# A post-norm decoder trunk on one core: the layer norms' statistics kept in PSUM, and the last norm in tile pairs

## The chip, the core and the metric

The kernel runs on one core of a Trainium2 chip. The core has five engines that work side by side: TensorE (PE in the rows; PEld is its weight load), VectorE (DVE), ScalarE (ACT), GpSimd (POOL) and SyncE (SP), which here issues the DMAs. Each engine takes its instructions strictly in the order in which they stand, and engines wait for each other through semaphores. Tiles lie in SBUF or, where TensorE writes its results, in the banks of PSUM. The metric is the device time of one execution in microseconds; lower is better.

## The reference

Two post-norm layers on x (256 tokens by 2048 features, float32): an RWKV-7 time mixing, a gated MLP, a causal differential attention, a gated MLP. Each of these four is followed by a layer norm.

```python
def layer_norm(x, g, b):
    mu = x.mean(-1, keepdims=True)
    var = jnp.square(x - mu).mean(-1, keepdims=True)
    return (x - mu) * lax.rsqrt(var + LN_EPS) * g + b

for i in range(DEPTH):                       # DEPTH = 2
    h = rwkv7_mix(x, ...) if i % 2 == 0 else diff_attn_mix(x, ...)
    x = layer_norm(ALPHA * x + h, ln_g[i, 0], ln_b[i, 0])
    x = layer_norm(ALPHA * x + conv_glu(x, ...), ln_g[i, 1], ln_b[i, 1])
```

## The kernel before

Activations lie transposed: features on the 128 partitions, the 256 tokens along a row. `X` holds the residual as 16 tiles of 128x256 (KT = 16). Every dense product is made in split precision. A weight chunk `raw` (128x512) comes by DMA; ScalarE rounds it to `hi` (L213), VectorE takes the rest `lo = raw - hi` (L216), each over 128x256, that is two k-tiles of 128. The activation is split the same way into `S` (L194 on ScalarE, L195 on VectorE). TensorE multiplies hi by both halves and lo by the high half (L228, L229, or in three narrow pieces). So a `lo` is wanted for every two k-tiles, and TensorE can run ahead of VectorE only as far as finished `lo` tiles reach.

The sums of a norm are made on TensorE by a product with a constant matrix (L348), into the two halves of one PSUM bank `lnst`: the mean in `sx`, the mean square in `sq`. `ln_stats` then lets ScalarE square the mean into `ln_m2` (L422) and copy the mean to SBUF as `ln_dm` (L423), VectorE form the variance `ln_v` (L424), ScalarE take Ln and Exp (L322, L323), and VectorE refine the result in three instructions (L324 to L326, a Newton step) into `ln_rs`, in SBUF.

The first three norms are hidden behind the next dense stage. An `Ahead` object makes the products of that stage's first six weight blocks with the tiles before they are normalized (L899 to L901, 16 k-tiles of six blocks) and mends the result afterwards in `total` with `ln_dm` and `ln_rs` (L307, L309). In between, `ln_apply` normalizes the 16 tiles: GpSimd subtracts the mean from all of them (L438), VectorE multiplies by `ln_rs` (L447, L455 or L460), ScalarE or VectorE applies scale and bias (L448, L456, L461, L462), and the tile is split again (L194, L195). All of this stands on the engines among the L213 and L216 rows of the running products. A scheduler writes the order on each engine out at build time, by its own estimates; nothing is reordered on the chip.

The fourth norm has nothing behind it: `ln_finish` subtracts the mean on VectorE (the tiles in `FIN_V`) and on GpSimd (the others, L475), multiplies by scale and `ln_rs` in one VectorE instruction (L483), adds the bias on ScalarE (L485) and sends two tiles at a time (L487).

Of the kernel before, what the change touches and what calls it, by code (L numbers as in the profile page):

```python
# [8 lines left out]
F32 = mybir.dt.float32  # L9
F32R = mybir.dt.float32r  # L10
AF = mybir.ActivationFunctionType
ALU = mybir.AluOpType
AX = mybir.AxisListType

P = 128
T = 256
D = 2048
KT = D // P
# [20 lines left out]
ORDER = [0, 1, 14, 2, 3, 4, 5, 6, 7, 15, 8, 9, 10, 11, 12, 13]  # L39
DBL = 64 * 16 + 16  # L40
LEAD = dict(q=9, p=(), e=1, a=1, s=4, n=0.301, d=8, h=0.1, r='ACAAAAAAAAAAABBB')
FIN_V = (0, 2, 5, 8, 11, 14)
FIN_S = range(2, KT + 1, 2)


def _param_layout():
# [82 lines left out]
class Trunk:  # L129
# [199 lines left out]
    def ln_begin(self, ahead=None, share=False):  # L329

        if self.ln_st is None:
            mk = lambda name, **k: self.ctx.enter_context(self.tc.tile_pool(name=name, bufs=1, side="right", **k))
            st = mk("lnst", space=bass.MemoryType.PSUM).tile([P, 2 * T], F32, name="lnst")
            self.ln_st = [st[:, :T], st[:, T:]]
            pool = mk("lnp")
            self.ln_dm, self.ln_rs, self.ln_c, self.ln_m2, self.ln_v = (
                pool.tile([P, T], F32, name=f"ln_{n}") for n in ("dm", "rs", "c", "m2", "v"))
            self.ln_sq = pool.tile([P, 4, T], F32, name="ln_sq")
            self.ln_acc = pool.tile([P, 2 * T], F32, name="ln_acc")
        self.ln_n, self.ln_open, self.ln_share, self.ln_first = 0, False, share, []  # L340
        self.ln_ahead, self.ln_last = ahead, []
        if ahead is not None:
            ahead.columns()
# [68 lines left out]
            nc.vector.tensor_tensor(out=x, in0=xa, in1=halves[0], op=ALU.add)  # L412
            self.ln_sums(j, n)

    def ln_stats(self):

        nc = self.nc
        sx, sq = self.ln_st
        self.ln_colsum((self.ln_acc[:, :T], self.ln_acc[:, T:]))
        for n, tiles in enumerate(self.ln_last):  # L420
            self.ln_colsum(tiles, n == len(self.ln_last) - 1)
        nc.scalar.activation(out=self.ln_m2, in_=sx, func=AF.Square)  # L422
        nc.scalar.copy(out=self.ln_dm, in_=sx)  # L423
        nc.vector.scalar_tensor_tensor(out=self.ln_v, in0=sq, scalar=LN_EPS, in1=self.ln_m2, op0=ALU.add,  # L424
                                       op1=ALU.subtract)
        self.rsqrt(self.ln_v, self.ln_rs, T, self.ln_m2)

    def ln_plain(self, i, h):
        self.ln_stats()
# [38 lines left out]

    def ln_finish(self, i, h, out):
        nc = self.nc  # L470
        at = 0

        def center(j):
            eng = nc.vector if j in FIN_V else nc.gpsimd
            eng.tensor_tensor(out=self.X[:, j, :], in0=self.X[:, j, :], in1=self.ln_dm, op=ALU.subtract)  # L475

        for j in range(-2, KT):
            if j < KT - 2:
                center(j + 2)
            if j < 0:  # L480
                continue
            x = self.X[:, j, :]
            nc.vector.scalar_tensor_tensor(out=x, in0=x, scalar=self.p(f"ln_g{i}{h}", j), in1=self.ln_rs, op0=ALU.mult,  # L483
                                           op1=ALU.mult)
            nc.scalar.activation(out=x, in_=x, func=AF.Identity, bias=self.p(f"ln_b{i}{h}", j))  # L485
            if j + 1 in FIN_S:
                nc.sync.dma_start(out=out[:, at:j + 1, :], in_=self.X[:, at:j + 1, :])  # L487
                at = j + 1

    def lead(self, feed, group, *args, ramp=0, ahead=4):  # L490

# [12 lines left out]
    def glu(self, i, lead, ahead=None, out=None):  # L504
        nc, tc = self.nc, self.tc
        with ExitStack() as ctx:
            self.weight_pools(ctx, f"g{i}")
            self.psum_pool(ctx, f"g{i}", 5)
            hp = ctx.enter_context(tc.tile_pool(name=f"glu_h{i}", bufs=1))
            gp_ = ctx.enter_context(tc.tile_pool(name=f"glu_t{i}", bufs=2))  # L510
            hs = hp.tile([P, FT, 2 * T], F32R, name="hs")
            gps = [hp.tile([P, T + 2], F32, name=f"gp{k}") for k in range(2)]
            for g in gps:
                nc.gpsimd.memset(g[:, 0:2], 0.0)
            cpar = hp.tile([P, 4 * FT], F32, name="cpar")
            nc.sync.dma_start(out=cpar, in_=self.a["par"][:, PCOL[f"cw{i}0"]:PCOL[f"cw{i}0"] + 4 * FT])
            cw = lambda k, j: cpar[:, k * FT + j:k * FT + j + 1]
            state = {}

            def evac(idx, ps):  # L520
                j = idx // 2
                if idx % 2 == 0:
                    g = gps[j % 2]
                    self.total(ps, g[:, 2:])
                    gc = gp_.tile([P, T], F32, name="gc")
                    nc.vector.tensor_scalar(out=gc, in0=g[:, 0:T], scalar1=cw(0, j),
                                            scalar2=cw(3, j), op0=ALU.mult, op1=ALU.add)
                    for k in (1, 2):
                        nc.vector.scalar_tensor_tensor(out=gc, in0=g[:, k:k + T], scalar=cw(k, j),
                                                       in1=gc, op0=ALU.mult, op1=ALU.add)  # L530
                    nc.scalar.activation(out=gc, in_=gc, func=AF.Gelu_apprx_tanh)
                    state[j] = gc
                else:
                    u = gp_.tile([P, T], F32, name="u")
                    self.total(ps, u)
                    nc.vector.tensor_tensor(out=u, in0=u, in1=state.pop(j), op=ALU.mult)
                    self.split(u, hs[:, j, :])

            blocks = self.up_blocks(i)
            n = 0  # L540
            if lead:
                n = len(lead.src)
                rest = lead.run(evac, [self.psum() for _ in lead.src])
                next(rest)
                if LEAD["e"] == 0:
                    _all(rest)
            for j, w in enumerate(blocks[n:]):
                def ev(_, ps, j=j):
                    if lead:
                        for _ in range(LEAD["e"]):  # L550
                            next(rest, None)
                    evac(j + n, ps)
                self.dense([w], KT, self.S0, ev)
            todo = self.bias_table() if i == 0 else iter(())
            self.ln_begin(ahead)
            for j in range(KT):
                if j in (1, 3, 5, 7, 9):
                    next(todo, None)
                last = j == KT - 1
                self.dense([self.a["ff_down"][i][j]], FT, hs, lambda _, ps: self.ln_add(j, ps, narrow=last, last=last),  # L560
                           narrow=last)
            if out is not None:
                self.ln_stats()
                self.ln_finish(i, 1, out)
            elif not ahead:
                self.ln_plain(i, 1)
# [366 lines left out]
def _all(steps):  # L933
    for _ in steps:
        pass
# [554 lines left out]
```

## Time and profile before

| | |
|---|---|
| three runs | 2544.0, 2544.87 and 2546.05 us; median 2544.87 |
| profiled execution | 2540.27 us, its span 2537.5 us, granted TensorE clock 0.99 |
| busy, TensorE | 2461.7 us (97%), its weight loads 2170.2 us |
| busy, VectorE / ScalarE / GpSimd | 2030.6 us (80%) / 1648.8 us (65%) / 172.0 us (7%) |
| the norms in the trace (L424 starts) | 662.99, 1394.15, 1793.29 and 2519.05 us |

Matmuls are pipelined, so the busy time of TensorE says little about idle time; the distance between starts does. A row of the timeline has the start, the duration, engine, line, operation, output and inputs, and in brackets how long the engine had been idle and what ended that.

### The profile page before, as it was taken

How to read it: one execution, taken by the hardware profiler on the slowest of the kernel's cores; microseconds unless marked ns; L12 is line 12 of the kernel's file. 1: busy time of each engine (PE TensorE's matmuls, PEld its weight loads, DVE VectorE, ACT ScalarE, POOL GpSimd, SP SyncE). 2: the span in 40 equal slices, each digit the busy share in tenths (PEclk: the TensorE clock that was granted, in tenths of full speed). 3: DMA queues.
4: the chain of work that ended last, by engine and by line, in shares of the span. 5: the costliest groups of instructions: out<-in, count | busy, mean ns of one | idle time of the engine just before them, and what ended most of it. 6: DMA issues, size and time to landing. Idle time of an engine off the chain costs nothing.

```text
span 2537.5 us, 56569 instructions
## 1 busy us (share of the span) xinstructions
PE 2461.7 (97%) x18622; PEld 2170.2 (86%) x18622; DVE 2030.6 (80%) x5192; ACT 1648.8 (65%) x4334; POOL 172.0 (7%) x236
## 2 busy tenths in 40 slices
PE   7999999999899999999999999999999999999996
PEld 6988888777888888888889899988988888888886
DVE  8988888878997777776776977779887777776776
ACT  5766566545676666665666666666766666666664
POOL 1000000000300000000111200003300000000111
PEclk9999999999999999999999999999999999999998
DMA  6644343344465556666766455556465555566664
GB/s 189 187 141 120 110 108 102 106 127 125 133 198 189 190 190 190 190 190 196 215 188 188 149 167 174 171 176 184 147 198 188 188 188 188 188 187 186 188 190 128
DMA packets 276743, 428.70 MB, mean 169 GB/s; under 512 B 60632, under 2 KB 83168, under 8 KB 276448
## 3 DMA queue, kind: packets, MB, share of 16 engines
q1 hardware_dynamic: 276448, 425.10, 55.6%
q8 instruction: 145, 2.38, 0.4%
q14 instruction: 150, 1.23, 0.2%
HBM read 420.25 MB, written 6.31 MB: 168 GB/s over the span
## 4 chain that ended last, share of the span: by engine, by line
PE 81%; DVE 3%; ACT 1%; DMA 1%; issue 1%; SPq 0%; POOL 0%; ACTq 0%; DVEq 0%; POOLq 0%
PE psd L228 43%; PE psd L229 22%; PE psd L224 2%; PE psd L225 2%; PE psd L226 2%; PE psd L296 1%; PE psd L295 1%; PE psd L294 1%; PE psd L900 1%; PE psd L899 1%; PE psd L901 1%; DVE lo L216 1%; DMA raw<-in_rw_o 1%; PE lnst L348 1%; PE pss L1152 0%
## 5 line engine op out<-in xcount | busy, mean ns | idle before, releaser
L213 ACT CAST hi<-raw 128x256 fp32r<-128x256 f32 (+1 forms) x3128 | 1231.4, 404 | 682.1 <-PE psd L228 466.2
L216 DVE TENSOR_TENSOR lo<-raw,hi 128x256 fp32r<-128x256 f32 (+1 forms) x3124 | 1308.3, 430 | 418.9 <-ACT hi L213 375.9
L228 PE MATMUL psd<-S,hi 128*128 128x512 f32 x3004 | 1056.7, 396 | 0.8 <-DVE S L195 0.8
L229 PE MATMUL psd<-S,lo 128*128 128x256 f32 x3004 | 842.1, 280 | 3.9 <-DVE lo L216 3.8
L228 PEld LDWEIGHTS psd<-S,hi 128*128 128x128 f32 x3004 | 566.2, 189 | 132.8 <-ACT hi L213 1.3
L229 PEld LDWEIGHTS psd<-S,lo 128*128 128x128 f32 x3004 | 566.0, 188 | 5.6 <-DVE lo L216 5.3
L228 PE MATMUL psd<-hs,hi 128*128 128x512 f32 x1290 | 451.2, 394 | 0.0
L229 PE MATMUL psd<-hs,lo 128*128 128x256 f32 x1290 | 361.5, 280 | 0.0
L228 PEld LDWEIGHTS psd<-hs,hi 128*128 128x128 f32 x1290 | 241.8, 187 | 56.3 <-ACT hi L213 0.9
L229 PEld LDWEIGHTS psd<-hs,lo 128*128 128x128 f32 x1290 | 243.1, 188 | 0.4 <-DVE lo L216 0.3
L226 PE MATMUL psd<-S,lo 128*128 128x256 f32 x480 | 139.1, 290 | 2.9 <-DVE lo L216 2.8
L224 PE MATMUL psd<-S,hi 128*128 128x256 f32 x480 | 138.5, 289 | 1.6 <-ACT hi L213 1.4
L225 PE MATMUL psd<-S,hi 128*128 128x256 f32 x480 | 137.6, 287 | 0.0
L228 PE MATMUL psd<-S1r,hi 128*128 128x512 f32 x276 | 107.2, 419 | 2.0 <-ACT hi L213 1.0
L226 PEld LDWEIGHTS psd<-S,lo 128*128 128x128 f32 x480 | 90.7, 189 | 8.6 <-DVE lo L216 5.0
L224 PEld LDWEIGHTS psd<-S,hi 128*128 128x128 f32 x480 | 90.7, 189 | 6.4 <-ACT hi L213 2.3
L225 PEld LDWEIGHTS psd<-S,hi 128*128 128x128 f32 x480 | 90.6, 189 | 1.7 <-issue 1.4
L366 POOL COPY ln_acc<-X 128x256 f32<-128x256 f32 x4 | 2.0, 512 | 1239.3 <-DVE X L400 1239.3
L224 PE MATMUL psd<-S1r,hi 128*128 128x256 f32 x284 | 85.6, 301 | 0.0
L900 PE MATMUL psd<-S,lo 128*128 128x258 f32 x256 | 77.7, 303 | 8.1 <-DVE lo L216 8.1
L228 PE MATMUL psd<-S1a,hi 128*128 128x512 f32 x240 | 84.9, 398 | 0.0
L229 PE MATMUL psd<-S1r,lo 128*128 128x256 f32 x276 | 80.8, 293 | 1.5 <-DVE lo L216 1.5
(303 smaller groups left out, 3577.3 us busy)
## 6 DMA issues: line engine op xcount, KB each, us to landing
raw<-in_ff_up SPq DMA_DIRECT2D x676, 256.0 KB, 3.4
raw<-in_ff_down SPq DMA_DIRECT2D x320, 256.0 KB, 3.0
raw<-in_rkv SPq DMA_DIRECT2D x192, 256.0 KB, 3.6
raw<-in_da_qk SPq DMA_DIRECT2D x122, 256.0 KB, 3.4
raw<-in_da_v SPq DMA_DIRECT2D x64, 256.0 KB, 3.0
raw<-in_da_o SPq DMA_DIRECT2D x64, 256.0 KB, 3.7
raw<-in_rw_o SPq DMA_DIRECT2D x50, 256.0 KB, 3.3
raw<-in_ff_down SPq DMA_DIRECT2D x32, 192.0 KB, 2.6
```

Source lines behind the costliest of these rows:

```text
L213: nc.scalar.copy(out=hi[:, :s * P], in_=r)
L216: eng.tensor_tensor(out=lo[:, :s * P], in0=r, in1=hi[:, :s * P].bitcast(F32), op=ALU.subtract)
L224: nc.tensor.matmul(ps[:, :T], lhsT=hi, rhs=xs[:, :T], start=first, stop=False)
L225: nc.tensor.matmul(ps[:, :T], lhsT=hi, rhs=xs[:, T:], start=False, stop=False)
L226: nc.tensor.matmul(ps[:, :T], lhsT=lo, rhs=xs[:, :T], start=False, stop=last)
L228: nc.tensor.matmul(ps, lhsT=hi, rhs=xs, start=first, stop=False)
L229: nc.tensor.matmul(ps[:, T:], lhsT=lo, rhs=xs[:, :T], start=False, stop=last)
L294: nc.tensor.matmul(o, lhsT=xh, rhs=hi, start=k == 0 and b == 0, stop=False)
L295: nc.tensor.matmul(o, lhsT=xh, rhs=lo, start=False, stop=False)
L296: nc.tensor.matmul(o, lhsT=xl, rhs=hi, start=False, stop=k == KT - 1 and b == T // P - 1)
L348: self.nc.tensor.matmul(st, lhsT=self.c("onesd"), rhs=t, start=not self.ln_open and n == 0, stop=stop and n == 1)
L900: nc.tensor.matmul(ps[:, 2:4 + T], lhsT=lo[:, w], rhs=x[:, 2:4 + T], start=False, stop=False)
```

## The change

`ln_begin` gives the names `ln_mean` and `ln_rs` to the two halves of the PSUM bank `lnst`; the SBUF tile for `ln_rs` is gone. `ln_stats` takes an optional function that is called after the variance, and spells out the reciprocal root with the result in that bank: ScalarE's Exp and VectorE's last refining instruction write it there, and the three instructions are written so that each reads the bank as one of its two inputs. Whatever multiplied by `ln_rs` in SBUF (L309, L447, L455, L460) now reads PSUM. GpSimd still subtracts `ln_dm`, the copy in SBUF.

`ln_finish` works on pairs of tiles. First come all subtractions: four pairs on VectorE, 128x512 at a time against `ln_mean` in PSUM, the eight tiles of the pairs in `FIN_P` on GpSimd. They are handed to `ln_stats`, so they stand ahead of Ln and Exp. Then, pair by pair, VectorE multiplies by `ln_rs` (128x512); scale and bias are one instruction per tile, on VectorE for the five tiles in the new `FIN_V` and on ScalarE for eleven. The pairs of `FIN_P` come last. Each pair is sent by itself, eight transfers as before.

```diff
-FIN_V = (0, 2, 5, 8, 11, 14)
-FIN_S = range(2, KT + 1, 2)
+FIN_P = (4, 6, 8, 10)
+FIN_V = (3, 7, 11, 13, 15)
...
-            self.ln_dm, self.ln_rs, self.ln_c, self.ln_m2, self.ln_v = (
-                pool.tile([P, T], F32, name=f"ln_{n}") for n in ("dm", "rs", "c", "m2", "v"))
+            self.ln_dm, self.ln_c, self.ln_m2, self.ln_v = (
+                pool.tile([P, T], F32, name=f"ln_{n}") for n in ("dm", "c", "m2", "v"))
+
+            self.ln_mean, self.ln_rs = self.ln_st
...
-    def ln_stats(self):
+    def ln_stats(self, then=None):
...
-        self.rsqrt(self.ln_v, self.ln_rs, T, self.ln_m2)
+        if then is not None:
+            then()
+        l, rs = self.ln_m2, self.ln_rs
+        nc.scalar.activation(out=l, in_=self.ln_v, func=AF.Ln)
+        nc.scalar.activation(out=rs, in_=l, func=AF.Exp, scale=-0.5)
+        nc.vector.tensor_tensor(out=l, in0=self.ln_v, in1=rs, op=ALU.mult)
+        nc.vector.scalar_tensor_tensor(out=l, in0=l, scalar=-0.5, in1=rs, op0=ALU.mult, op1=ALU.mult)
+        nc.vector.scalar_tensor_tensor(out=rs, in0=l, scalar=1.5, in1=rs, op0=ALU.add, op1=ALU.mult)
...
     def ln_finish(self, i, h, out):
-        for j in range(-2, KT):
-            if j < KT - 2:
-                center(j + 2)
-            ...
-            nc.vector.scalar_tensor_tensor(out=x, in0=x, scalar=self.p(f"ln_g{i}{h}", j), in1=self.ln_rs, op0=ALU.mult,
-                                           op1=ALU.mult)
-            nc.scalar.activation(out=x, in_=x, func=AF.Identity, bias=self.p(f"ln_b{i}{h}", j))
-            if j + 1 in FIN_S:
-                nc.sync.dma_start(out=out[:, at:j + 1, :], in_=self.X[:, at:j + 1, :])
+        wide = lambda t: t.unsqueeze(1).broadcast_to([P, 2, T])
+        g, b = (lambda j: self.p(f"ln_g{i}{h}", j)), (lambda j: self.p(f"ln_b{i}{h}", j))
+
+        def center():
+            for j in range(0, KT, 2):
+                xs = self.X[:, j:j + 2, :]
+                if j in FIN_P:
+                    for k in range(2):
+                        nc.gpsimd.tensor_tensor(out=xs[:, k], in0=xs[:, k], in1=self.ln_dm, op=ALU.subtract)
+                else:
+                    nc.vector.tensor_tensor(out=xs, in0=xs, in1=wide(self.ln_mean), op=ALU.subtract)
+
+        self.ln_stats(center)
+        for j in [j for j in range(0, KT, 2) if j not in FIN_P] + list(FIN_P):
+            xs = self.X[:, j:j + 2, :]
+            nc.vector.tensor_tensor(out=xs, in0=xs, in1=wide(self.ln_rs), op=ALU.mult)
+            for k in (j, j + 1):
+                x = self.X[:, k, :]
+                if k in FIN_V:
+                    nc.vector.tensor_scalar(out=x, in0=x, scalar1=g(k), scalar2=b(k), op0=ALU.mult, op1=ALU.add)
+                else:
+                    nc.scalar.activation(out=x, in_=x, func=AF.Identity, scale=g(k), bias=b(k))
+            nc.sync.dma_start(out=out[:, j:j + 2, :], in_=xs)
```

The new program numbers the lines behind these edits higher by up to 13: L447 of before is L456 after, L455 is L464, L456 is L465. VectorE in the first norm, from the refining instructions on, before (`ln_m` is the tile `ln_m2`):

```order
L324 TENSOR_TENSOR ln_m_9945<-ln_rs 128x256 [waits Activation_49]
L216 TENSOR_TENSOR lo<-raw,hi 128x256 [waits DMAHW0_49,DVE_49,Activation_49]
L325 SCALAR_TENSOR_TENSOR ln_m_9945<-ln_m_9945,ln_v 128x256 [waits DVE_49]
L216 TENSOR_TENSOR lo<-raw,hi 128x256 [waits Activation_49]
L326 SCALAR_TENSOR_TENSOR ln_rs<-ln_m_9945,ln_rs 128x256 [waits DVE_49]
L216 TENSOR_TENSOR lo<-raw,hi 128x256 [waits DMAHW1_49,Activation_49]
L447 TENSOR_TENSOR X<-X,ln_rs 128x256 [waits DVE_49,Pool_49]
L455 TENSOR_TENSOR X<-X,ln_rs 128x256 [waits Pool_49]
L216 TENSOR_TENSOR lo<-raw,hi 128x256 [waits Activation_49]
L456 TENSOR_SCALAR X<-X,par 128x256 [waits DVE_49]
L447 TENSOR_TENSOR X<-X,ln_rs 128x256 [waits Pool_49]
L216 TENSOR_TENSOR lo<-raw,hi 128x256 [waits DMAHW2_49,Activation_49]
```

The same place after, where `lnst` is the PSUM bank:

```order
L433 TENSOR_TENSOR ln_m_9944<-ln_v,lnst 128x256 [waits DVE_49,Activation_49]
L216 TENSOR_TENSOR lo<-raw,hi 128x256 [waits DMAHW0_49,Activation_49]
L434 SCALAR_TENSOR_TENSOR ln_m_9944<-ln_m_9944,lnst 128x256 [waits DVE_49]
L216 TENSOR_TENSOR lo<-raw,hi 128x256 [waits Activation_49]
L435 SCALAR_TENSOR_TENSOR lnst<-ln_m_9944,lnst 128x256 [waits DVE_49]
L216 TENSOR_TENSOR lo<-raw,hi 128x256 [waits DMAHW1_49,Activation_49]
L456 TENSOR_TENSOR X<-X,lnst 128x256 [waits DVE_49,Pool_49]
L464 TENSOR_TENSOR X<-X,lnst 128x256 [waits Pool_49]
L216 TENSOR_TENSOR lo<-raw,hi 128x256 [waits Activation_49]
L465 TENSOR_SCALAR X<-X,par 128x256 [waits DVE_49]
L216 TENSOR_TENSOR lo<-raw,hi 128x256 [waits DMAHW2_49,Activation_49]
L195 TENSOR_TENSOR S_76<-X,S_76 128x256 [waits Activation_49] x2
```

The rows stand almost as before, with other inputs; the second L447 has moved behind the next L216 and two L195 (and a further L216, not shown). In the last norm two more places moved. ScalarE, after, from the copy of the mean on:

```order
L425 COPY ln_dm<-lnst 128x256
L431 ACTIVATE ln_m_9944<-ln_v 128x256 [waits DVE_49]
L432 ACTIVATE lnst<-ln_m_9944 128x256 [waits DVE_49,Activation_49]
L501 ACTIVATE X<-X,par 128x256 [waits DVE_49]
L501 ACTIVATE X<-X,par 128x256
```

Exp (L432) has a wait for VectorE that its counterpart L323 does not have before: the count that it waits for is reached when the fourth of the subtractions below is done. VectorE there, after:

```order
L426 SCALAR_TENSOR_TENSOR ln_v<-lnst,ln_m_9944 128x256 [waits PE_49,Activation_49]
L490 TENSOR_TENSOR X<-X,lnst 128x512 x3
L490 TENSOR_TENSOR X<-X,lnst 128x512 [waits DVE_49,Pool_49]
L433 TENSOR_TENSOR ln_m_9944<-ln_v,lnst 128x256 [waits Activation_49]
L434 SCALAR_TENSOR_TENSOR ln_m_9944<-ln_m_9944,lnst 128x256 [waits DVE_49]
L435 SCALAR_TENSOR_TENSOR lnst<-ln_m_9944,lnst 128x256 [waits DVE_49]
L495 TENSOR_TENSOR X<-X,lnst 128x512 [waits DVE_49]
L495 TENSOR_TENSOR X<-X,lnst 128x512 x2
L499 TENSOR_SCALAR X<-X,par 128x256 [waits DVE_49] x2
```

Here all subtractions of VectorE stand ahead of the refining instructions; before, three stood there and three between them.

More of the change, by code (lines that the diff above doesn't have):

```diff
@@ L470, in ln_finish @@
         nc = self.nc
[L471 to L475, printed above, removed]
-        for j in range(-2, KT):
-            if j < KT - 2:
-                center(j + 2)
[L480 to L483, printed above, removed]
-                                           op1=ALU.mult)
-            nc.scalar.activation(out=x, in_=x, func=AF.Identity, bias=self.p(f"ln_b{i}{h}", j))
-            if j + 1 in FIN_S:
-                nc.sync.dma_start(out=out[:, at:j + 1, :], in_=self.X[:, at:j + 1, :])
-                at = j + 1
+        wide = lambda t: t.unsqueeze(1).broadcast_to([P, 2, T])
[19 more added lines that the diff above has]
+            nc.sync.dma_start(out=out[:, j:j + 2, :], in_=xs)
     def lead(self, feed, group, *args, ramp=0, ahead=4):
@@ L562, in glu @@
             if out is not None:
-                self.ln_stats()
                 self.ln_finish(i, 1, out)
```

## The prediction

> **What bounds the kernel now.** I read the page first (span, chain of waits), then TensorE's waits around each norm, then the timelines there.
>
> ```profile
> span 2537.5 us, 56569 instructions
> PE 81%; DVE 3%; ACT 1%; DMA 1%; issue 1%; SPq 0%; POOL 0%; ACTq 0%; DVEq 0%; POOLq 0%
> ```
>
> TensorE carries 81% of the chain, so a norm counts only where TensorE stands still. The busy times by stretch (columns: stretch, length, then PE, PEld, DVE, ACT, POOL busy with instruction counts, granted clock, DMA share, GB/s) show how long. The first three run from the matmul at which TensorE first lacks a `lo` to the end of the six early blocks, one stretch for each of the first three norms.
>
> ```profile
> 671.72:696.16 24.44, 21.36 (x150) 20.85 (x151) 23.84 (x62) 19.46 (x57) 6.31 (x7) 0.86 0.47 131
> 1402.88:1426.90 24.02, 20.93 (x150) 20.32 (x149) 23.09 (x59) 19.32 (x58) 5.82 (x7) 0.86 0.42 123
> 1801.99:1826.19 24.20, 21.09 (x151) 20.59 (x151) 23.57 (x60) 19.64 (x58) 6.50 (x7) 0.86 0.45 132
> ...
> 672.00:676.00 4.00, 1.63 (x9) 1.43 (x10) 4.00 (x5) 2.53 (x8) 4.00 (x6) 0.93 0.21 66
> 677.40:680.00 2.60, 2.58 (x12) 2.58 (x13) 2.60 (x9) 2.26 (x7) 0.00 (x0) 0.50 0.25 70
> 682.30:686.00 3.70, 3.70 (x33) 3.70 (x32) 3.70 (x12) 3.70 (x11) 0.00 (x0) 1.00 0.41 106
> ```
> ```profile
> 671.44 0.28 PE L899 MATMUL psd<-S,hi 128*128 128x260 f32 x1
> 672.88 0.39 PE L900 MATMUL psd<-S,lo 128*128 128x258 f32 x1 [1.16 <-DVE lo L216]
> 675.35 0.56 PE L900 MATMUL psd<-S,lo 128*128 128x258 f32 x1 [1.49 <-DVE lo L216]
> 677.42 0.58 PE L900 MATMUL psd<-S,lo 128*128 128x258 f32 x1 [0.44 <-DVE lo L216]
> ...
> 682.41 0.29 PE L899 MATMUL psd<-S,hi 128*128 128x260 f32 x1
> 682.53 0.28 PE L900 MATMUL psd<-S,lo 128*128 128x258 f32 x1
> ```
>
> At full clock matmuls start 0.12 us apart (682.41, 682.53); 150 take 18.0 us. The three stretches took 24.4, 24.0 and 24.2, so each norm costs TensorE about 6.2 us, 18.7 in all. Half is waiting for `lo` (1.16 + 1.49 + 0.44), the rest the clock: 0.50 after the waits. VectorE meanwhile never rests:
>
> ```profile
> 664.87 0.95 DVE L324 TENSOR_TENSOR ln_m<-ln_rs 128x256 f32<-128x256 f32 x1
> 665.74 0.95 DVE L216 TENSOR_TENSOR lo<-raw,hi 128x256 fp32r<-128x256 f32 x1
> ...
> 675.22 1.81 DVE L195 TENSOR_TENSOR S<-X,S 128x256 fp32r<-128x256 f32 x2
> 676.95 0.41 DVE L216 TENSOR_TENSOR lo<-raw,hi 128x256 fp32r<-128x256 f32 x1
> 677.29 0.41 DVE L447 TENSOR_TENSOR X<-X,ln_rs 128x256 f32<-128x256 f32 x1
> ```
> ```profile
> 663.03 13.71 POOL L438 TENSOR_TENSOR X<-X,ln_dm 128x256 f32<-128x256 f32 x16 [12.24 <-ACT ln_dm L423]
> ```
>
> While GpSimd subtracts (663.03 to 676.74), VectorE's rows start 0.87 us apart; once it has ended, 0.34 apart (676.95, 677.29). The engines take turns: GpSimd's turn is 0.87 - 0.34 = 0.53 us. Whether a PSUM input escapes this is the question, and earlier rows answer it:
>
> ```profile
> 641.94 0.95 DVE L411 TENSOR_TENSOR t<-X,ln_c 128x256 f32<-128x256 f32 x1
> 642.82 0.41 DVE L409 TENSOR_TENSOR t<-t,psd 128x256 f32<-128x256 f32 x1
> 643.15 0.74 DVE L412 TENSOR_TENSOR X<-t,psd 128x256 f32<-128x256 f32 x2
> ```
> ```profile
> 641.83 0.79 POOL L373 TENSOR_TENSOR ln_acc<-ln_acc,X 128x256 f32<-128x256 f32 x1 [2.82 <-DVE X L412]
> 642.58 0.92 POOL L373 TENSOR_TENSOR ln_acc<-ln_acc,t 128x256 f32<-128x256 f32 x1
> ```
>
> GpSimd works from 641.83 to 643.50. L411, both inputs in SBUF, takes 0.95; L409, one input in PSUM (`psd`), 0.41 in the midst of it, and the pair of L412 starts 0.33 later at full pace.
>
> **The first three norms.** The new order, priced with 0.87 for a row with both inputs in SBUF while GpSimd works and nothing for one with a PSUM input, which fits into GpSimd's turn (0.34 against 0.53). In the first norm, from 664.87 to the `lo` that starts at 676.95, nine SBUF rows stand: L216, L216, L216, L216, L465, L216, L195 twice, L216. That is 9 x 0.87 = 7.8, and 0.5 for a further turn that GpSimd gets under the adjoining L456 and L464: the `lo` is done at about 673.2 instead of 677.36. TensorE uses up a `lo` in 6 x 0.12 = 0.72 us and would want this one, the third since 671.72, at 673.16: almost no wait. GpSimd itself ends at 663.03 + 16 x 0.53 + 14 x 0.34 = 676.3, hardly earlier, since VectorE's SBUF rows still take turns with it. From there VectorE needs 0.34 a row. The `lo` that comes latest is the eleventh, twelve rows on: 676.3 + 12 x 0.34 = 680.4, wanted at 671.72 + 10 x 0.72 = 678.9. Later ones are 1.0 to 1.4 late. So TensorE waits 1.5 us in small pieces instead of 3.1 in two blocks, and what is late next is still a `lo`.
>
> Does the clock hold? A stretch in which TensorE was thinly fed:
>
> ```profile
> 176.00:180.00 4.00, 2.71 (x26) 2.41 (x25) 4.00 (x11) 2.74 (x7) 0.00 (x0) 1.00 0.36 112
> ```
>
> Busy 2.71 of 4 us left it at 1.00, while 1.63 of 4 (672 to 676) lost it. With 1.5 us of waits over seven it should hold. So a norm loses 1.5 instead of 6.2: a gain of 4.9 in the first (24.44 - 18.0 - 1.5) and 4.7 in the third. In the second, something waits behind the products:
>
> ```profile
> 1427.62 0.36 PE L294 MATMUL psd<-hi,S 128*128 128x256 f32 x1 [0.61 <-DVE lw L928]
> ```
>
> VectorE reaches that L928 only some 3.4 us earlier by the same count, so I take 3.5. Sum 13.1. Bounds: nothing (the `lo` rows come no earlier) and 18.7 (no loss left). I take the upper part because the two prices are measured in the very place.
>
> No row shows ScalarE or VectorE writing a result into PSUM, as L432 and L435 do. The nearest, Exp into SBUF, takes 0.42 (below); I take 0.42. Six such rows stand in three norms; at 0.95 they would cost 3 us, at nothing they gain 2.5.
>
> **The last norm.** Nothing covers it; every step counts.
>
> ```profile
> 2519.05 0.42 DVE L424 SCALAR_TENSOR_TENSOR ln_v<-lnst,ln_m 128x256 f32<-128x256 f32 x1 [1.98 <-ACT ln_dm L423]
> 2519.39 2.44 DVE L475 TENSOR_TENSOR X<-X,ln_dm 128x256 f32<-128x256 f32 x3
> ...
> 2526.93 6.88 DVE L483 SCALAR_TENSOR_TENSOR X<-X,par,ln_rs 128x256 f32<-128x256 f32 x16
> ```
> ```profile
> 2519.96 0.42 ACT L323 ACTIVATE ln_rs<-ln_m 128x256 f32<-128x256 f32 x1
> 2527.90 6.49 ACT L485 ACTIVATE X<-X,par 128x256 f32<-128x256 f32 x16 [7.53 <-DVE X L483]
> ```
> ```profile
> 1439.60 0.68 DVE L662 SCALAR_TENSOR_TENSOR s<-pss,B 128x512 f32<-128x512 f32 x1
> 1440.31 0.69 DVE L666 TENSOR_REDUCE mx<-s 128x2 f32<-128x512 f32 x1
> 1440.91 0.75 DVE L216 TENSOR_TENSOR lo<-raw,hi 128x256 fp32r<-128x256 f32 x2
> ```
> ```profile
> 677.74 0.60 ACT L448 ACTIVATE X<-X,par 128x256 f32<-128x256 f32 x1 [1.76 <-DVE X L447]
> 678.25 0.70 ACT L213 CAST hi<-raw 128x256 fp32r<-128x256 f32 x2
> ```
> ```profile
> 672.75 0.82 DVE L456 TENSOR_SCALAR X<-X,par 128x256 f32<-128x256 f32 x1
> 673.49 0.95 DVE L447 TENSOR_TENSOR X<-X,ln_rs 128x256 f32<-128x256 f32 x1
> ```
>
> Before, compute ends at 2527.90 + 6.49 = 2534.4. Prices: a 128x512 row 0.60 to the next start and 0.69 in all (L666); a row that needs the one just ahead starts 0.03 after its end (1440.31); ScalarE with scale and bias 0.51 (677.74 to 678.25). After: `ln_v` at 2519.05; four pairs 2519.39 to 2521.9. Exp waits for them now: 2522.4. That wait puts 2.0 us on Exp against 2520.4 before, and VectorE, whose next row is the first refining one, idles for half a microsecond of it. Three refining rows of 0.45, not 0.87 to 1.7 with a subtraction between: 2523.7, where before the first multiplication starts at 2526.93. Then eight multiplications (0.60) and the tiles' scale and bias (0.34): the last pair starts at 2523.7 + 7 x 0.60 + 4 x 0.34 = 2529.3, is done at 2530.0, ScalarE ends its tile at 2530.6. GpSimd's eight subtractions (0.53 each, from the copy's end at about 2519.1) end by 2523.4, ahead of need. Gain 3.8; the eight transfers now follow each other faster, for which I take 0.3 off: 3.5. Bounds: with VectorE's scale and bias at the 0.74 that it shows beside GpSimd (672.75 to 673.49), 1.5; with ScalarE at its 0.41 a tile, 4.2.
>
> [...]
>
> **Sum.** 13.1 + 3.5 = 16.6. Against the profiled execution (2540.27, 2.8 around its span) 2523.7; it is 4.6 below the median of the runs, so the runs should give 2544.87 - 16.6 = 2528.3.
>
> **Rivals.** (B) The clock falls all the same. It was low from 675.35 to 682.2; 6.8 us at half pace cost 3.0, with 0.8 of waits 3.8 a norm: gain 2.4 x 3 + 3.5 = 10.7, 2534.2. For it: 2.65 us of waits in 4 were enough. Against: 176 to 180. [...] (C) The PSUM input does not escape. The three norms stay; the last, with pairs at 0.60 + 0.53, ends within 0.5 of 2534.4: 2544.9. Only L409 and L412 speak against it. (D) Slower: `lnst`, written by ScalarE and VectorE, reads slower than a bank that TensorE wrote. Ninety rows read or write it (25 in each of three norms, 15 in the last); it decides from 0.24 us a row, and at twice 0.41 the loss is 37 - 16.6 = 20: 2565. Against it stands L424, which reads the same bank in 0.42.
>
> **How the numbers follow.** Forecast 0.70, B 0.18, C 0.08, D 0.04. About 0.2%, 5.1 us, is what a measurement of this kernel tells from no change. Forecast and B are faster: 0.88; C the same: 0.08; D slower: 0.04. Range: below, 18.7 + 4.2 gained, 2522; above, B with the last norm at its lower bound, 7.2 + 1.5, 2536. C and D, 0.12, lie outside.
>
> **What would show it.** Right: L456 and L433 to L435 at about 0.42 beside GpSimd; the three stretches near 19.5 us at clock 1.00; last compute at 2530.6 less what the norms gained. Wrong: L456 at 0.95 (C), a clock of 0.5 behind the waits (B), rows of L495 well above 0.7 (D). The forecast fails most easily where ScalarE's L213 or L194 come late to a VectorE that runs ahead; their queue is nearly full behind 677.74.

## The result, and the profile after

The changed kernel took 2529.72 us (median of 4 runs, 2528.06 to 2531.07), against 2545.45 for the kernel before: ratio 0.9939, 95% interval 0.9921 to 0.9956. Forecast were 2528.3 and a range of 2522 to 2536, so the time came out as said. That flatters the forecast: two later timings of the same kernel gave ratios of 0.9963 (0.9951 to 0.9975) and 0.9966 (0.9953 to 0.9980), 9.4 and 8.6 us; all three intervals hold a gain of 11.2 to 12.0 us.

The profiled execution took 2531.07 us, its span 2529.3. A single span says little, because the recurrence ahead of the first norm, which the change doesn't touch, ends at another time in each execution: the first `ln_v` of the changed kernel starts at 666.9, 670.1 and 669.1 us in its three profiles. The same four microseconds in the recurrence, busy times by stretch, before and after (TensorE, its weight load, VectorE, ScalarE, GpSimd, then the granted clock):

```profile
384.00:388.00 4.00, 3.73 (x30) 2.91 (x28) 3.81 (x13) 3.69 (x9) 0.00 (x0) 1.00 0.14 48
```
```profile
384.00:388.00 4.00, 4.00 (x37) 2.90 (x34) 2.05 (x7) 2.07 (x5) 0.00 (x0) 0.50 0.17 61
```

The clock was 1.00 in one execution and 0.50 in the other. Up to the first `ln_v` VectorE, ScalarE, GpSimd and TensorE (its matmuls) run the same instructions in the same order in all eleven profiles of this document, and `ln_v` tends to come later the longer the clock was halved ahead of it: at 659.3 us behind 10.2 us of half clock, at 671.3 behind 41.0. What is behind the recurrence repeats closely, so I count from the first `ln_v`. The rows of that instruction (shortest, median and longest duration in ns, then first and last start), before and after:

```profile
L424 DVE SCALAR_TENSOR_TENSOR ln_v<-lnst,ln_m x4: 425/425/425, 663.0 to 2519.1; 128x256 f32<-128x256 f32 x4
```
```profile
L426 DVE SCALAR_TENSOR_TENSOR ln_v<-lnst,ln_m x4: 425/425/426, 666.9 to 2514.4; 128x256 f32<-128x256 f32 x4
```

| us, profiled executions | before | after | gain |
|---|---|---|---|
| first to fourth `ln_v` (the first three norms) | 1856.1 | 1847.5 | 8.5 |
| fourth `ln_v` to the span's end (the last norm) | 18.5 | 14.9 | 3.6 |
| sum | 1874.5 | 1862.4 | 12.1 |

In the two later profiles of the changed kernel the sum is 1863.2 and 1862.4.

Busy times by stretch, after, for the three stretches that the prediction took (each from 8.73 us behind `ln_v` to the end of the early products):

```profile
675.59:696.00 20.41, 19.69 (x150) 18.22 (x149) 20.05 (x51) 16.94 (x47) 5.08 (x7) 1.00 0.48 130
1402.76:1423.84 21.08, 19.81 (x149) 18.16 (x148) 19.97 (x52) 17.07 (x49) 5.08 (x7) 1.00 0.45 128
1800.20:1820.73 20.53, 19.88 (x151) 18.31 (x149) 19.56 (x50) 16.18 (x44) 4.97 (x6) 1.00 0.42 122
```

They were 24.4, 24.0 and 24.2 us at a mean clock of 0.86; now 20.4, 21.1 and 20.5 at 1.00. TensorE's waits of over 0.2 us in the first of them (timeline; in brackets the idle time and what ended it):

```profile
677.34 0.38 PE L913 MATMUL psd<-S,lo 128*128 128x258 f32 x1 [0.33 <-DVE lo L216]
681.19 0.39 PE L913 MATMUL psd<-S,lo 128*128 128x258 f32 x1 [0.23 <-DVE lo L216]
```

Two short waits stand where 1.16, 1.49 and 0.44 stood. VectorE and GpSimd there:

```profile
671.38 0.41 DVE L456 TENSOR_TENSOR X<-X,lnst 128x256 f32<-128x256 f32 x1
671.71 0.41 DVE L464 TENSOR_TENSOR X<-X,lnst 128x256 f32<-128x256 f32 x1
672.04 0.99 DVE L216 TENSOR_TENSOR lo<-raw,hi 128x256 fp32r<-128x256 f32 x1
672.95 0.82 DVE L465 TENSOR_SCALAR X<-X,par 128x256 f32<-128x256 f32 x1
673.69 0.96 DVE L216 TENSOR_TENSOR lo<-raw,hi 128x256 fp32r<-128x256 f32 x1
...
676.33 0.96 DVE L216 TENSOR_TENSOR lo<-raw,hi 128x256 fp32r<-128x256 f32 x1
677.21 0.41 DVE L456 TENSOR_TENSOR X<-X,lnst 128x256 f32<-128x256 f32 x1
```
```profile
666.90 13.62 POOL L447 TENSOR_TENSOR X<-X,ln_dm 128x256 f32<-128x256 f32 x16 [11.94 <-ACT ln_dm L425]
```

L456 and L464 take 0.41 in the midst of GpSimd's work, where L447 and L455 of before took 0.95. The rows with two SBUF inputs still take turns: L216 took 0.99 and 0.96 there, 0.41 once GpSimd had ended (680.73). L465, a TENSOR_SCALAR with one tile in SBUF, took 0.82 to 0.83 all the same, in each of the three norms; its like in the last norm, L499, took 0.40 to 0.41 with GpSimd at rest. Why it pays beside GpSimd no run here shows.

The last norm, VectorE and ScalarE, after:

```profile
2514.39 0.42 DVE L426 SCALAR_TENSOR_TENSOR ln_v<-lnst,ln_m 128x256 f32<-128x256 f32 x1 [1.98 <-ACT ln_dm L425]
2514.73 2.47 DVE L490 TENSOR_TENSOR X<-X,lnst 128x512 f32<-128x512 f32 x4
2517.72 0.42 DVE L433 TENSOR_TENSOR ln_m<-ln_v,lnst 128x256 f32<-128x256 f32 x1 [0.51 <-ACT lnst L432]
...
2519.09 1.88 DVE L495 TENSOR_TENSOR X<-X,lnst 128x512 f32<-128x512 f32 x3
```
```profile
2517.29 0.39 ACT L432 ACTIVATE lnst<-ln_m 128x256 f32<-128x256 f32 x1 [2.03 <-DVE X L490]
...
2522.31 3.64 ACT L501 ACTIVATE X<-X,par 128x256 f32<-128x256 f32 x7 [0.42 <-DVE X L495]
```

The first multiplication starts 4.70 us behind `ln_v` (7.88 before), the last compute ends 11.56 behind it (15.34 before).

### The profile page after: what moved, and what is told of

Read it like the earlier page. It is cut to its first block, busy times and chain, and to the rows that moved or that the text cites. A ratio compares the mean times of both kernels' runs of the same rounds, so it can differ in the third digit from the quotient of the medians.

```text
span 2529.3 us, 56543 instructions
## 1 busy us (share of the span) xinstructions
PE 2462.5 (97%) x18622; PEld 2168.1 (86%) x18622; DVE 2018.1 (80%) x5187; ACT 1650.5 (65%) x4329; POOL 166.1 (7%) x234
## 4 chain that ended last, share of the span: by engine, by line
PE 82%; DVE 3%; ACT 1%; DMA 1%; issue 1%; POOL 0%; ACTq 0%; DVEq 0%; POOLq 0%
PE psd L228 43%; PE psd L229 22%; PE psd L224 2%; PE psd L225 2%; PE psd L226 2%; PE psd L295 1%; PE psd L294 1%; PE psd L296 1%; DVE lo L216 1%; PE lnst L350 1%; PE psd L913 1%; PE psd L914 1%; PE psd L912 0%; PE pss L1165 0%; DVE S L195 0%
## 5 line engine op out<-in xcount | busy, mean ns | idle before, releaser
L216 DVE TENSOR_TENSOR lo<-raw,hi 128x256 fp32r<-128x256 f32 (+1 forms) x3124 | 1309.7, 430 | 417.4 <-ACT hi L213 379.9
L229 PE MATMUL psd<-S1r,lo 128*128 128x256 f32 x276 | 81.3, 295 | 1.8 <-DVE lo L216 1.8
L226 PE MATMUL psd<-S1r,lo 128*128 128x256 f32 x284 | 80.7, 284 | 1.7 <-DVE lo L216 1.5
```

The source lines that it names most:

```text
L216: eng.tensor_tensor(out=lo[:, :s * P], in0=r, in1=hi[:, :s * P].bitcast(F32), op=ALU.subtract)
L226: nc.tensor.matmul(ps[:, :T], lhsT=lo, rhs=xs[:, :T], start=False, stop=last)
L229: nc.tensor.matmul(ps[:, T:], lhsT=lo, rhs=xs[:, :T], start=False, stop=last)
```

## The experiments

Times are compared with the kernel before in the same turns, and the microseconds behind a ratio are worked out from it; the trace's measure, from the first `ln_v` to the span's end, stands beside it. The diffs are against the changed kernel and show the lines that matter, not every one; the comments in them are not in the kernels.

**Only the last norm changed.** The first three keep the reciprocal in SBUF:

```diff
-        if then is not None:
-            then()
-        l, rs = self.ln_m2, self.ln_rs
+        if then is None:
+            self.rsqrt(self.ln_v, self.ln_rs, T, self.ln_m2)     # ln_rs in SBUF
+            return
+        then()
+        l, rs = self.ln_m2, self.ln_rp                           # ln_rp in PSUM
```

> The changed kernel with the first three norms as before: there the reciprocal deviation is made and kept in SBUF; only the last norm uses PSUM, pairs and the new order. Theory (the gain has two parts that add: rows with a PSUM input do not take turns with GpSimd in the first three norms, and the new last norm): the three stretches lose about 6.2 us each as before and show the clock of 0.50 again; from ln_v to the last compute in the last norm about 11.6 us instead of 15.3; time 3.5 us under before, near 2542. Rival (the parts lean on each other: the last norm gains only because the first three ones changed what reaches it, or the reverse): the last norm takes over 13 us or the time is more than 7 us under before.

Ratio 0.9979 (0.9968 to 0.9989), 5.3 us; by the trace 1870.0, 4.5 under before, of which 3.6 in the last norm. The other 0.9 comes in norms whose half clock lasted 3.4 us instead of 6.8. TensorE's waits in the first norm, and a stretch behind them:

```profile
674.83 0.39 PE L915 MATMUL psd<-S,lo 128*128 128x258 f32 x1 [1.17 <-DVE lo L216]
677.30 0.39 PE L915 MATMUL psd<-S,lo 128*128 128x258 f32 x1 [1.47 <-DVE lo L216]
679.38 0.58 PE L915 MATMUL psd<-S,lo 128*128 128x258 f32 x1 [1.09 <-DVE lo L216]
```
```profile
679.20:682.60 3.40, 3.22 (x15) 3.22 (x16) 3.40 (x11) 2.91 (x9) 0.00 (x0) 0.51 0.28 77
```

The waits and the half clock are back, so what took them away in the changed kernel is in the first three norms' part.

**Only the first three norms changed.** The last norm has the loop that the change takes out (`ln_finish` of before, not shown), and reads the reciprocal in PSUM:

```diff
             if out is not None:
+                self.ln_stats()
                 self.ln_finish(i, 1, out)
```

> The changed kernel with the last norm's loop of before (it reads the mean in SBUF and the reciprocal in PSUM). Theory: the three stretches as in the changed kernel, 20.5 to 21.4 us for the 150 matmuls with the clock at 1.00; the last norm 14.5 to 15.3 us; time 9 to 13 us under before, 2532 to 2536. Rival (most of the gain is the last norm's): less than 6 us under before.

Ratio 0.9964 (0.9951 to 0.9977), 9.1 us, as expected; by the trace 1862.7, 11.9 under before. The first three norms give 8.8, the changed kernel's 8.5 within 0.3. The last norm was a miss: its last compute ends 12.3 us behind `ln_v`, not 14.5 to 15.3, and its span's end 15.4 behind, where it was 18.5 before. VectorE there:

```profile
2506.51 0.42 DVE L426 SCALAR_TENSOR_TENSOR ln_v<-lnst,ln_m 128x256 f32<-128x256 f32 x1 [1.98 <-ACT ln_dm L425]
2506.86 2.44 DVE L484 TENSOR_TENSOR X<-X,ln_dm 128x256 f32<-128x256 f32 x3
2509.22 0.41 DVE L433 TENSOR_TENSOR ln_m<-ln_v,lnst 128x256 f32<-128x256 f32 x1
2509.55 0.61 DVE L484 TENSOR_TENSOR X<-X,ln_dm 128x256 f32<-128x256 f32 x1
2510.08 0.41 DVE L434 SCALAR_TENSOR_TENSOR ln_m<-ln_m,lnst 128x256 f32<-128x256 f32 x1
...
2511.81 6.34 DVE L492 SCALAR_TENSOR_TENSOR X<-X,par,lnst 128x256 f32<-128x256 f32 x16
```

Each refining row (0.41) fits into GpSimd's turn, and the subtraction behind it then takes 0.61. So the first multiplication starts 5.3 us behind `ln_v` instead of 7.88. Of the last norm's 3.6 us, 3.1 come with the place of the reciprocal alone; pairs, order and sharing add 0.5.

**Only the refining rows read PSUM** in the first three norms; the last of them writes SBUF, and the multiplications read that:

```diff
+        to = self.ln_rs if then is None else rs                  # SBUF in the first three
-        nc.vector.scalar_tensor_tensor(out=rs, in0=l, scalar=1.5, in1=rs, op0=ALU.add, op1=ALU.mult)
+        nc.vector.scalar_tensor_tensor(out=to, in0=l, scalar=1.5, in1=rs, op0=ALU.add, op1=ALU.mult)
```

> The changed kernel, but the last refining row of the first three norms writes the reciprocal into SBUF, so that only the refining rows have PSUM inputs there and all multiplications by it have two SBUF inputs. Theory (each row with two SBUF inputs costs 0.87 beside GpSimd, one with a PSUM input 0.34 inside GpSimd's turn): L456 and L464 take 0.95 again; the third late lo comes some 12.4 us behind ln_v (14.4 before, 10.4 changed), so TensorE waits about 2.2 us in the first stretch, in pieces of up to 1.3. If the clock then holds, a stretch loses 3 to 4 us and the time is 9 to 11 under before; if it falls to 0.50, a stretch loses 5 to 6 and the time is 4 to 7 under before. Rival (the order of the rows, not the place of the operands, brought the gain): L456 at 0.95, yet stretches as in the changed kernel and a time within 2 us of it.

Ratio 0.9963 (0.9951 to 0.9976), 9.4 us; by the trace 1867.3, 7.2 under before and 4.9 above the changed kernel. First norm, VectorE, TensorE's waits (and those of the second norm), and the stretches behind the first:

```profile
666.75 0.95 DVE L457 TENSOR_TENSOR X<-X,ln_rs 128x256 f32<-128x256 f32 x1
667.62 0.96 DVE L465 TENSOR_TENSOR X<-X,ln_rs 128x256 f32<-128x256 f32 x1
```
```profile
672.01 0.39 PE L914 MATMUL psd<-S,lo 128*128 128x258 f32 x1 [0.34 <-DVE lo L216]
674.62 0.39 PE L914 MATMUL psd<-S,lo 128*128 128x258 f32 x1 [1.63 <-DVE lo L216]
676.35 0.39 PE L914 MATMUL psd<-S,lo 128*128 128x258 f32 x1 [0.76 <-DVE lo L216]
...
1404.19 0.39 PE L914 MATMUL psd<-S,lo 128*128 128x258 f32 x1 [1.62 <-DVE lo L216]
1405.93 0.38 PE L914 MATMUL psd<-S,lo 128*128 128x258 f32 x1 [0.76 <-DVE lo L216]
```
```profile
677.20:680.00 2.80, 2.80 (x15) 2.80 (x15) 2.80 (x10) 2.66 (x8) 0.00 (x0) 0.50 0.33 94
680.00:682.80 2.80, 2.80 (x25) 2.80 (x25) 2.80 (x9) 2.80 (x9) 0.00 (x0) 0.98 0.34 89
```

The late `lo` starts TensorE 12.4 us behind `ln_v`, as worked out; the waits come to 2.7 us instead of 2.2. The clock fell in the first and the third norm; in the second it stayed at 1.00 through the same waits (0.34 at 1401.59, then the two shown). The stretches lose 4.8, 4.8 and 4.2 us, so the second loses as much with its clock as the first without. From `ln_v` to the last early product the first norm takes 32.9 us before, 31.3 here and 28.85 changed: with fewer PSUM inputs the loss grows, though the rows stand in much the same order. The rival, that the order did it, falls by the trace alone. The timing does not tell this kernel from the changed one (9.4 each), as the rival had it; one profile of this kernel stands 4.1 to 4.9 us above the three of the changed one.

**The changed kernel again.**

> The changed kernel itself, timed in the same turns as the three kernels that undo or keep parts of it. If the parts add, its gain over before is the sum of those of the kernel with only the last norm changed and of the one with only the first three changed, within the intervals: 12 to 17 us, 2529 to 2533.

Ratio 0.9963, 9.4 us, less than the 12 to 17 expected. The two parts don't simply add (5.3 and 9.1, or 4.5 and 11.9 by the trace): the last norm's 3.1 us are in both.

**VectorE subtracts in the first three norms**, from the mean in PSUM; GpSimd rests:

```diff
-            nc.gpsimd.tensor_tensor(out=self.X[:, j, :], in0=self.X[:, j, :], in1=self.ln_dm, op=ALU.subtract)
+            nc.vector.tensor_tensor(out=self.X[:, j, :], in0=self.X[:, j, :], in1=self.ln_mean, op=ALU.subtract)
```

> The changed kernel, but in the first three norms VectorE itself subtracts the mean, from PSUM, in all 16 tiles; GpSimd has no row there, so no turns are left. Sixteen rows of 0.34 are added to VectorE (5.4 us a norm); in the changed kernel GpSimd's turns held VectorE up for about 5 us of its 13.6. Theory (what is left of the loss is VectorE's number of rows, turns or not): no wait for a lo in the first 15 us behind ln_v, but the same loss or more towards the end of the six early blocks, where the postponed rows fall; from ln_v to the last of the early products 29 to 31 us in the first and third norm and up to 34 in the second, time from that of the changed kernel to 8 us above it. Rival (the turns with GpSimd are all that is left): 27 to 27.5 us in all three and a time about 5 us under the changed kernel.

Ratio 1.0006 (0.9994 to 1.0019): the whole gain is gone, by the trace too (1874.5, 12.0 above the changed kernel, where 8 at most was expected). The last early product starts 26.2 us behind `ln_v` in all three norms, with no wait ahead of it: sooner than the theory (29 to 34) and even the rival (27 to 27.5) had it. Then VectorE has the postponed rows to do, and TensorE stands still (first norm; then the clock):

```profile
702.82 0.40 PE L229 MATMUL psd<-S,lo 128*128 128x256 f32 x1 [4.81 <-DVE lo L216]
```
```profile
703.00:707.00 4.00, 4.00 (x15) 3.43 (x16) 4.00 (x14) 1.23 (x3) 2.02 (x2) 0.57 0.48 153
```

So the rival was right on the early products: without turns they run free, and 26.2 is what they take with no loss. The theory was right that VectorE's number of rows is what is left, but not on the place and the size: the loss falls behind the early products, and sixteen more rows on a VectorE that is busy throughout cost more than the turns did. That holds for the order in which the scheduler put them; no other was tried.

**One pair ahead in the last norm:**

```diff
-        self.ln_stats(center)
+        self.ln_stats(lambda: center(rest[:1] + list(FIN_P)))
...
             nc.vector.tensor_tensor(out=xs, in0=xs, in1=wide(self.ln_rs), op=ALU.mult)
+            center(rest[n + 1:n + 2])
```

> The changed kernel, but in the last norm only one of VectorE's four pairs is subtracted ahead of Ln and Exp; the others follow one by one behind the products. Theory (Exp waits for every earlier VectorE row that reads its bank): Exp starts 0.05 us behind the first subtraction, 1.0 us behind ln_v instead of 2.9; the refining rows start 1.5 us behind ln_v instead of 3.3, the first pair goes out 1.9 us sooner, but VectorE has as much work as before and the last compute comes at 11.3 to 11.6 us behind ln_v (11.56 in the changed kernel). Rival (Exp waits for something else): Exp still starts 2.9 us behind ln_v.

This kernel and the next were run once each and are read by the trace. Exp (L432) starts 1.1 us behind `ln_v`, right behind the one subtraction; its wait is what the order showed. `ln_v` is at 2519.88:

```profile
2520.99 0.39 ACT L432 ACTIVATE lnst<-ln_m 128x256 f32<-128x256 f32 x1 [0.24 <-DVE X L490]
```

The last compute comes 11.7 us behind `ln_v`, the span's end 15.0: nothing gained. The wait of 2.03 us on Exp costs nothing, because VectorE, which has as much work either way, used the time.

**The last norm shared anew**, on top of that edit:

```diff
-FIN_P = (4, 6, 8, 10)
-FIN_V = (3, 7, 11, 13, 15)
+FIN_P = (4, 6, 8, 10, 12)
+FIN_V = (5, 9, 13)
```

> As the kernel with one pair ahead, and in the last norm GpSimd subtracts five pairs instead of four and ScalarE does the scale and bias of 13 tiles instead of 11. By the prices of the trace (0.60 a 128x512 row, 0.34 and 0.52 a tile on VectorE and ScalarE) ScalarE ends 10.5 us behind ln_v, 1.0 sooner than in the changed kernel. Theory (compute sets the end): the span ends 13.9 us behind ln_v instead of 14.9. Rival (the eight transfers set it, since they follow each other without a gap in the changed kernel): the span still ends 14.6 to 14.9 us behind ln_v.

ScalarE ends at 2526.25, 10.9 us behind `ln_v` (2515.38), and the span 14.2 behind (expected 10.5 and 13.9), 0.7 sooner than in the changed kernel:

```profile
2521.72 4.53 ACT L503 ACTIVATE X<-X,par 128x256 f32<-128x256 f32 x9 [0.29 <-DVE X L496]
```

Compute sets the end; the transfers follow 3.3 us behind the last compute in both.

**Products ahead in the first three norms**, with the last norm of the kernel above:

```diff
-        for j in range(-2, KT):
-            if j < KT - 2:
-                center(j + 2)
+        for j in range(-2 - 4, KT):
+            if j < KT - 2 - 4:
+                center(j + 2 + 4)
+            if -4 <= j < KT - 4:
+                times(j + 4)
```

`times` is the multiplication by `ln_rs`, taken out of the branches below; besides, `n` in `LEAD` goes from 0.301 to 0.2.

> The changed kernel with the last norm shared anew (one pair ahead, five pairs subtracted by GpSimd, 13 tiles' scale and bias on ScalarE) and, in the first three norms, the multiplications by the reciprocal issued four tiles ahead of the rest of each tile, with the tiles spread more slowly over the early products (0.2 tiles a step instead of 0.301). Theory (a row with a PSUM input costs nothing beside GpSimd, so the more of them stand there the less is lost): by 0.87 and 0.34 a row the later lo tiles of the early products come about 1 us sooner than in the changed kernel; from ln_v to the last early product 27.9 to 28.6 us instead of 28.9, the span's end 14.2 us behind the last ln_v instead of 14.9; 1 to 3 us under the changed kernel. Rival (the order in the changed kernel is already the better one, because the first lo tiles then come later): 29 us or more, and no gain.

> The changed kernel once more, in the same turns as the kernel with the products ahead: 9 to 13 us under before (12.1 by the two profiled executions, counted from the first ln_v on).

The products ahead: 2523.43 us (2522.0 to 2528.15), ratio 0.9941 (0.9929 to 0.9954). The changed kernel in the same turns: 2533.01, ratio 0.9966 (0.9953 to 0.9980), 8.6 us under before and a little less than expected. By the trace 1859.5 against 1862.4 (12.1 under before, as expected), 2.9 us better: 2.3 in the first three norms, the rest in the last, which the kernel above had changed. The medians differ by more; in these two profiles the part ahead of the first norm brings in 2.2 us, and what brings in the rest is not shown. By the trace it is the fastest of the kernels here. VectorE in its first norm:

```profile
671.44 1.73 DVE L454 TENSOR_TENSOR X<-X,lnst 128x256 f32<-128x256 f32 x5
...
675.33 2.71 DVE L216 TENSOR_TENSOR lo<-raw,hi 128x256 fp32r<-128x256 f32 x3
```

Five products in a row cost 1.7 us beside GpSimd; TensorE waits once, for 0.76 us, and the clock stays. From `ln_v` to the last early product it takes 28.3, 28.8 and 28.2 us (27.9 to 28.6 expected), against 28.6, 30.3 and 28.7 in the changed kernel beside it. How much of that the order brings, and how much the slower spread, was not tried apart.

## Why the prediction was right, and where it was not

- **The price of a row** was right: 0.41 for L456 and 0.41 to 0.42 for L433 to L435 beside GpSimd, 0.82 to 0.99 for the others, but 0.62 or 0.63 for an L216 right behind one of L433 to L435. The third `lo` was done at 677.3, forecast 673.2 on a clock that stood 3.9 us earlier, that is 677.1. Rivals C and D fall with it: rows on a bank that ScalarE and VectorE wrote take 0.41 as well, and Exp into PSUM took 0.39. L424, which was set against D, does not bear on it: it reads what TensorE wrote.
- **GpSimd** ended 13.6 us behind its start against 13.3 forecast: hardly sooner, as said.
- **The clock** held at 1.00 in all three norms, so rival B falls: TensorE is busy for 2.7 us or more in any 3.4 us of them (in the two later profiles for 2.0 or more). The ground given for that, 2.71 us busy of 4, was a weak one: elsewhere in the same trace the clock fell at 2.78 of 3.41, and the waits of 2.7 us with only the refining rows changed cost it in two norms of three (last section). Nor does the clock's loss simply add to the waits, as B's price has it: with only the last norm changed the half clock lasted half as long, the third wait grew from 0.44 to 1.09, and the three norms gained 0.9 us in all.
- **"A norm loses 1.5"** is the term that was mis-sized. By the same arithmetic the stretches lose 2.4, 3.1 and 2.5 (20.41 - 18.0, and so on). In the first only 0.56 of it are waits of over 0.2 us; the rest are matmuls with a `lo` that start a little late one by one, behind a VectorE without slack (busy for 20.05 of the 20.41 us). So the stretches gain 4.0, 2.9 and 3.7 us, and some of that is given back behind the early products, where the sum had no loss for the first and third norm: from one `ln_v` to the next the gain is 4.0, 1.65 and 2.9, together 8.5 where 4.9, 3.5 and 4.7 were forecast, 13.1. VectorE still has postponed rows there, and TensorE waits for a `lo`, in the second norm and in the third, where it did not before:

```profile
1429.03 0.39 PE L295 MATMUL psd<-lo,S 128*128 128x256 f32 x1 [0.94 <-DVE lo L216]
```
```profile
1821.28 0.39 PE L229 MATMUL psd<-S,lo 128*128 128x256 f32 x1 [0.32 <-DVE lo L216]
```

- **A transfer** that the forecast didn't look at adds to it in the second norm. In the 20 us from `ln_v` the DMA brings 55 to 121 GB/s here in the first two norms (stretches of 4 us), in the 12 us behind them 159 to 252. There a `raw` comes late to ScalarE, and so `hi` to TensorE (0.52 us here, 1.29 and 1.25 in the two later profiles):

```profile
1416.86 0.41 ACT L213 CAST hi<-raw 128x256 fp32r<-128x256 f32 x1 [0.90 <-DMA raw<-in_da_qk]
```
```profile
1418.24 0.38 PE L912 MATMUL pss<-S,hi 128*128 128x260 f32 x1 [0.52 <-ACT hi L213]
```

- **The second norm's smaller share**, put down to L928 (L941 after), came out smaller than said: TensorE still waits 0.59 us for it, but the norm gained 1.65 us (0.9 and 1.5 in the two later profiles) and not 3.5; the late transfer and the wait of 0.94 us stand against it.
- **The last norm** was right to 0.1 us at the steps that count: first multiplication 4.70 us behind `ln_v` (4.65), last compute 11.56 (11.55), gain 3.6 (3.5). GpSimd's eight subtractions took 5.5 us and not 4.3, which cost nothing, because its tiles come last. What the gain was put down to was not right: most of it is the refining rows' escape from GpSimd, which needs none of the pairs and the new order.
- **The sum** of 16.6 is 12.1 in the trace. That the first medians differ by 15.7, close to the forecast, is luck: the two later ratios give 9.4 and 8.6. The part ahead of the first norm scatters by more than the 3.6 us between 15.7 and 12.1 (the first `ln_v` starts at 659.3 to 672.6 us), but what it did in the runs without a profile is not shown.

## What to carry to other kernels

Where VectorE and GpSimd work at once, look at where each VectorE row's two inputs lie: with one of them in PSUM, a row of 0.41 us stood beside GpSimd for nothing here, with both in SBUF it cost 0.87. Then place such rows where GpSimd works, which gave another 2.3 us, together with a slower spread; moving GpSimd's work to a VectorE that is busy throughout gave the whole gain back. Measure an effect of half a percent from a point behind the part that scatters, with the trace beside the medians.

## What the runs showed of the hardware that was not expected

The half clock comes in pieces of one length or a multiple of it: about 3.4 us in the kernel with only the last norm changed (679.3 to 682.7) and in the one with only the refining rows changed (676.7 to 680.1), 6.8 us before (675.4 to 682.2), and 10.2 us before, in the recurrence (525.2 to 535.5). The pieces also start whole steps of one length apart: after, in the recurrence, at 381.22, 432.42, 483.62 and 510.93 us, which is 15, 15 and 8 steps of 3.4133 us; before, from 525.22 on, at 651.51, 675.41, 1405.86 and 1805.22, which is 37, 7, 214 and 117. Whether thin feeding costs the clock depends on when it comes. Busy times by stretch with only the refining rows changed: ahead of the loss in the first norm and in it; two stretches of the second norm, 212 and 213 steps behind that loss (676.71); and the thinnest 3.4 us of the second norm:

```profile
673.30:676.71 3.41, 1.33 (x9) 1.13 (x10) 3.41 (x6) 1.24 (x4) 2.72 (x4) 1.00 0.13 38
676.71:680.12 3.41, 3.41 (x18) 3.41 (x17) 3.41 (x11) 3.05 (x9) 0.00 (x0) 0.50 0.27 77
1400.34:1403.75 3.41, 1.89 (x14) 1.47 (x12) 3.41 (x5) 1.69 (x5) 3.41 (x5) 1.00 0.17 61
1403.75:1407.16 3.41, 2.21 (x16) 2.01 (x17) 3.41 (x8) 1.75 (x5) 1.85 (x3) 1.00 0.14 38
1402.60:1406.00 3.40, 1.05 (x7) 0.85 (x7) 3.40 (x5) 0.96 (x3) 3.00 (x4) 1.00 0.13 38
```

With TensorE busy for 1.05 us of 3.4 the clock stayed in the second norm; counted in steps, the thin part is split there between two, of 1.89 and 2.21. In the first norm 1.33 lay within one step, and the clock was lost. The loss in the third norm, at 1803.11, lies 330 such steps behind the first. Counted so, in all eleven profiles from the first `ln_v` to the last, every loss comes behind a step with 0 to 1.44 us busy (1.04, 1.41 and 1.16 in the three norms before), and no step with less than 1.78 kept the clock. So the clock also fell behind steps in which TensorE worked for over 1 us. But busy time alone does not set the limit. In the recurrence, before, the clock fell behind 2.78 us of it, in 96 short matmuls:

```profile
521.81:525.22 3.41, 2.78 (x96) 2.06 (x85) 1.92 (x5) 0.91 (x4) 0.00 (x0) 1.00 0.21 17
525.22:535.46 10.24, 10.24 (x97) 6.67 (x96) 5.79 (x15) 4.63 (x12) 0.00 (x0) 0.50 0.37 100
```

What is counted in a step, where the limit lies, and why a piece lasts one step or several, stays open.
